# Gate and up projections of a second block's feed forwards as seven block products per pair of columns, with weights in pieces of 1024 columns

## The chip, the cores and the metric

The kernel runs on one core of a Trainium2 chip. The metric is device time in microseconds of one execution. PE is TensorE, DVE is VectorE, ACT is ScalarE, POOL is GpSimd, SP is SyncE, which issues the weight transfers here.

## The reference, cut to what matters

Two transformer blocks of two layers each run over 512 tokens of width 1024. Every layer ends in a feed forward of inner width 2816. The first block's has a causal convolution on the gate half, the second block's has none:

```python
def swiglu(h, w_gate_up, w_down):
    g, u = jnp.split(h @ w_gate_up, 2, axis=-1)
    return (jax.nn.silu(g) * u) @ w_down
...
        x = x + swiglu(rmsnorm_2(x, norm_ffn_g[layer]), ffn_w_gate_up[layer], ffn_w_down[layer])
```

Inputs, weights and output are float32.

## The kernel before

x lies transposed: 8 tiles of 128 features by 512 tokens. A float32 operand is split into a rounded half hi (ACT, L111 for weights) and a remainder lo (DVE, L112, which reads raw and hi from SBUF), and each product of tiles is three matmuls: hi by xh, hi by xl, lo by xh (`mm3`, L217 to L219). The norm's per-token factor Rb is multiplied in when a PSUM bank is read.

Weights come in chunks of 1024 rows by 256 columns (2048 columns in SBUF) in the order in which `make_plan` lists them. Three raw buffers and two hi/lo pairs rotate. `next` hands out a chunk; `pump`, called after every unit of 24 matmuls by `tick`, splits the chunk that follows in four pieces of 512 columns and loads ahead on SP's queue. `tick` then reads the finished bank (the `ev` functions) and lets each background generator (`bg`, `step`) do one step.

`ffn` goes over the 22 inner tiles of 128 in three parts (`FPARTS`, 8, 8 and 6 tiles). For each pair of tiles it takes a gate chunk `fa` and a value chunk `fv`, each as two units of 8 row tiles by 3 matmuls of 512 columns. `ev_a` multiplies by Rb (DVE, L870), applies silu (ACT, L880) and multiplies by Rb again (POOL, L881); `ev_v` multiplies by the value (DVE, L885) and splits the result (L229, L230). After a part the down chunks `fd` multiply its tiles and `x_add` adds to x (DVE, L536). The first pair of a feed forward straddles the norm (`first_pair`, `norm_gen`). The last layer's last part is `down_final`, in halves of 256 tokens, so with matmuls of 256 columns, and with the output behind it.

Every engine runs its instructions in the order of the program. The tile framework puts in the waits: an instruction waits for the tiles that it reads, and for the readers of a buffer that it overwrites. PSUM has eight banks, handed out in turn.

## Time and profile before

| | us |
|---|---|
| median of 3 runs | 2755.0 (2753.39 to 2757.13) |
| the profiled execution | 2753.09 |
| its span, first to last instruction | 2751.3 |
| PE busy in the span | 2719.3 |
| DVE, ACT, POOL busy | 1483.1, 1047.7, 335.6 |
| mean granted TensorE clock | 0.997 |

The span is what the trace shows; 1.8 us of the execution lie outside it. A matmul's own duration overlaps the next one's, so the price of a matmul is read from start to start. The feed forwards of the second block start at about 1650 and 2350 us of the span.

### The profile page before, as it was taken

Reading aid. Unit: us, or ns where it says so; the run is one execution under the profiler, and the core shown is the slowest. Engines: PE = TensorE matmul, PEld = TensorE weight load, DVE = VectorE, ACT = ScalarE, POOL = GpSimd, SP = SyncE. Lnnn points to the kernel's source line nnn. Section 1 sums busy time; section 2 is a strip of 40 time slices with the busy share of each in tenths; the row PEclk is TensorE's granted clock in tenths of the full one; section 3 lists DMA queues with packets and bytes.
Section 4 is the critical chain, followed back from the end, with each engine's and each line's share of the span. In section 5 each row is a group of like instructions: output and inputs, shape, how many; then the busy total and the mean of one; then the engine's idle time right before and its main releaser. Section 6 shows DMA issues by size and latency. Waiting matters only on the chain.

```text
span 2751.3 us, 33428 instructions
## 1 busy us (share of the span) xinstructions
PE 2719.3 (99%) x13358; PEld 2265.2 (82%) x13358; DVE 1483.1 (54%) x2533; ACT 1047.7 (38%) x1967; POOL 335.6 (12%) x394
## 2 busy tenths in 40 slices
PE   9999999999999999999999999999999999999998
PEld 7788888888878888888888887888888888788887
DVE  5644764545555375645466666434466656543444
ACT  5353343323445334423343354222243536432223
POOL 1110210101111011100021102000111001100002
PEclk9999999999999999999999999999999999999999
DMA  5131323232323133223233223332232112322321
GB/s 190 62 93 54 115 92 103 87 101 82 115 65 84 63 100 107 98 88 106 85 100 111 93 76 127 99 100 92 81 99 78 62 47 85 115 92 95 105 85 54
DMA packets 254269, 253.55 MB, mean 92 GB/s; under 512 B 16384, under 2 KB 252160, under 8 KB 253600
## 3 DMA queue, kind: packets, MB, share of 16 engines
q1 hardware_dynamic: 251808, 245.68, 27.6%
q0 software_dynamic: 1296, 4.92, 0.5%
q8 instruction: 105, 1.72, 0.3%
q10 hardware_dynamic: 1008, 0.80, 0.1%
q14 instruction: 52, 0.43, 0.0%
HBM read 247.15 MB, written 2.10 MB: 91 GB/s over the span
## 4 chain that ended last, share of the span: by engine, by line
PE 93%; DVE 4%; ACT 2%; issue 1%; POOL 0%; DMA 0%; POOLq 0%; ACTq 0%; DVEq 0%
PE ps L217 28%; PE ps L218 28%; PE ps L219 28%; DVE lo L112 1%; PE ps L828 1%; PE ps L730 1%; PE ps L1436 1%; PE ps L673 1%; DVE x L536 0%; PE ps L1160 0%; PE ps L843 0%; PE ps L451 0%; PE ps L754 0%; PE ps L460 0%; ACT xh L232 0%
## 5 line engine op out<-in xcount | busy, mean ns | idle before, releaser
L217 PE MATMUL ps<-xh,hi 128*128 128x512 f32 x2224 | 872.9, 392 | 5.1 <-ACT hi L111 5.1
L219 PE MATMUL ps<-xh,lo 128*128 128x512 f32 x2224 | 866.8, 390 | 1.6 <-DVE lo L112 1.5
L218 PE MATMUL ps<-xl,hi 128*128 128x512 f32 x2224 | 866.5, 390 | 0.0
L112 DVE TENSOR_TENSOR lo<-raw,hi 128x512 fp32r<-128x512 f32 (+2 forms) x922 | 635.8, 746 | 157.9 <-ACT hi L111 156.5
L111 ACT ACTIVATE hi<-raw 128x512 fp32r<-128x512 f32 (+2 forms) x922 | 506.6, 618 | 323.5 <-PE ps L218 254.2
L217 PEld LDWEIGHTS ps<-xh,hi 128*128 128x128 f32 x2224 | 418.0, 188 | 93.7 <-ACT hi L111 5.9
L219 PEld LDWEIGHTS ps<-xh,lo 128*128 128x128 f32 x2224 | 417.8, 188 | 90.7 <-DVE lo L112 3.4
L218 PEld LDWEIGHTS ps<-xl,hi 128*128 128x128 f32 x2224 | 418.0, 188 | 85.2 <-issue 0.2
L218 PE MATMUL ps<-actl,hi 128*128 128x512 f32 (+1 forms) x752 | 282.4, 376 | 0.3 <-DVE actl L230 0.3
L217 PE MATMUL ps<-acth,hi 128*128 128x512 f32 (+1 forms) x752 | 282.5, 376 | 0.0
L219 PE MATMUL ps<-acth,lo 128*128 128x512 f32 (+1 forms) x752 | 282.3, 375 | 0.0
L536 DVE TENSOR_TENSOR x<-ps,x 128x512 f32<-128x512 f32 x136 | 93.4, 688 | 266.5 <-PE ps L219 266.5
L218 PEld LDWEIGHTS ps<-actl,hi 128*128 128x128 f32 x752 | 141.5, 188 | 26.1 <-DVE actl L230 0.5
L217 PEld LDWEIGHTS ps<-acth,hi 128*128 128x128 f32 x752 | 141.5, 188 | 25.7
L219 PEld LDWEIGHTS ps<-acth,lo 128*128 128x128 f32 x752 | 141.5, 188 | 25.5
L870 DVE TENSOR_TENSOR a<-ps,Rb 128x512 f32<-128x512 f32 x88 | 60.6, 691 | 180.6 <-PE ps L219 173.1
L417 POOL TENSOR_TENSOR sq<-sq,sq 128x512 f32<-128x512 f32 (+1 forms) x73 | 94.7, 1302 | 436.4 <-ACT sq L411 435.9
L881 POOL TENSOR_TENSOR y<-y,Rb 128x512 f32<-128x512 f32 x44 | 57.0, 1297 | 588.2 <-ACT y L877 588.2
L881 POOL TENSOR_TENSOR a<-a,Rb 128x512 f32<-128x512 f32 x44 | 58.0, 1321 | 571.2 <-ACT a L880 571.2
L217 PE MATMUL ps<-hi,xh 128*128 128x256 f32 x384 | 113.4, 295 | 0.0
L218 PE MATMUL ps<-lo,xh 128*128 128x256 f32 x384 | 108.5, 283 | 0.0
L232 ACT ACTIVATE xh<-x,prm 128x512 fp32r<-128x512 f32 x72 | 52.0, 725 | 148.3 <-DVE x L536 145.8
(367 smaller groups left out, 3157.3 us busy)
## 6 DMA issues: line engine op xcount, KB each, us to landing
raw<-in_w_up SPq DMA_DIRECT2D x44, 1024.0 KB, 5.1
raw<-in_ffn_w_gate_up SPq DMA_DIRECT2D x44, 1024.0 KB, 5.1
raw<-in_w_in SPq DMA_DIRECT2D x39, 1024.0 KB, 5.1
raw<-in_w_down SPq DMA_DIRECT2D x16, 1024.0 KB, 5.1
raw<-in_ffn_w_down SPq DMA_DIRECT2D x16, 1024.0 KB, 5.1
raw<-in_od_w_in SPq DMA_DIRECT2D x10, 1024.0 KB, 5.2
raw<-in_w_o SPq DMA_DIRECT2D x8, 1024.0 KB, 5.1
raw<-in_xattn_wkv SPq DMA_DIRECT2D x8, 1024.0 KB, 5.1
```

Source lines behind the costliest of these rows:

```text
L111: nc.scalar.activation(g(hi, d), g(raw, s), AF.Copy)
L112: nc.vector.tensor_tensor(g(lo, d), g(raw, s), g(hi, d).bitcast(F32), op=SUB)
L217: mm(out, lhsT=wh, rhs=xh, start=first, stop=False)
L218: mm(out, lhsT=wh, rhs=xl, start=False, stop=False)
L219: mm(out, lhsT=wl, rhs=xh, start=False, stop=last)
L232: nc.scalar.activation(hv, src, AF.Copy, scale=scale)
L417: (nc.vector if dve else nc.gpsimd).tensor_tensor(acc[to], acc[to], q, op=ADD)
L536: self.nc.vector.tensor_tensor(self.x[j], ps, self.x[j], op=ADD)
L673: nc.tensor.matmul(z[b][:, o:o + n], lhsT=k[rs, kt * P:(kt + 1) * P], rhs=q[rs, kt * P:S], start=(kt != 3), stop=False, skip_group_check=True)
L730: nc.tensor.matmul(po[rs, kt * P:S], lhsT=vb[:, kt, h * 64:(h + 1) * 64], rhs=ag[kt], start=(kt == 0), stop=(kt == 3))
L870: nc.vector.tensor_tensor(t, ps, self.Rb, op=MUL)
L881: nc.gpsimd.tensor_tensor(t, t, self.Rb, op=MUL)
```

## The change

Only the second block's feed forwards compute differently. Their first two pairs of tiles stay as they were; for f from 4 on (`PLAIN`), the four blocks of a pair (gate and value columns by the upper and lower 512 rows) and the four blocks of the normalised x (upper and lower rows by the first and second 256 tokens) are combined by the scheme of Winograd's form of Strassen's product: seven products of blocks with sums before and after, in place of eight.

- The x side is formed once per feed forward by `factors`, a background generator: per j one scaling of two tiles by ACT, their multiplication by Rb and four sums of 256 columns on POOL, then splits on ACT and DVE. It is stepped in the ticks of the pairs 0 and 2, and yields `ready` after six steps.
- The weight side is formed for every pair by `schunks`: POOL sums in place on the raw tiles (`pre` two, `post1` one, `post5` one, 1024 columns each), and seven splits of 1024 columns, one for each product.
- `product` runs 24 matmuls of 256 columns on a bank. `spair` reads the banks: copies by ACT, sums by DVE, silu by ACT, and half of the multiplication by the value on POOL. The seventh product of a pair runs behind the first of the next, or behind the first down unit of a part.
- All weights of the kernel, in every stage, come in units of 1024 columns: six raw buffers and four hi/lo pairs of that size, one ACT and one DVE instruction per unit, `pump` by units.
- All down-projections but the last come as pieces of 2 row tiles by 512 columns, with four banks open at a time. There are four parts instead of three, of 6, 6, 4 and 6 tiles, in the last feed forward 6, 6, 6 and 4.
- Pools are opened and closed by stage, and the bias table of the first block is loaded twice.

```diff
+    RAW, HL = 6, 4
...
+    def may_emit(self):
+        i = self.emitted
+        if i >= len(self.units) or i >= self.limit:
+            return False
+        held = sum(1 for k in range(self.base, i) if not self.units[k]["own"])
+        return self.units[i]["own"] or held < self.HL
+    def pump(self, n=None):
+        n = self.pace if n is None else n
+        while n > 0 and self.may_emit():
+            self._emit()
+            n -= 1
+        while self.loaded < min(len(self.raws), self.freed + self.RAW):
+            self._load()
+    pace = 2
...
+def schunks(name, w, c1, c2):
+    b = [block(w, r, 4, c, 256) for r, c in ((0, c1), (0, c2), (512, c2), (512, c1))]
+    b11, b12, b22, b21 = b
+    box = {}
+    def add(c, to, x, y):
+        c.nc.gpsimd.tensor_tensor(to, x, y, op=ADD)
+    def pre(c, r):
+        box["t"] = c.pf.tile([P, 1024], F32, tag="t0", bufs=1, name=c.nm("t0")).rearrange("p (k c) -> p k c", k=4)
+        add(c, box["t"], r[0], r[1])
+        add(c, r[1], r[1], r[2])
+    def post1(c, r):
+        add(c, r[0], r[0], r[1])
+    def post5(c, r):
+        add(c, r[0], r[0], r[1])
+    def temp(c, hi, lo, raws):
+        c.put(hi, lo, box.pop("t"))
+    u = [dict(unit(4, 256, whole, (b11,), 0), pre=pre, praws=(b11, b12, b22), post=post1),
+         unit(4, 256, temp, (b11,), 0),
+         unit(4, 256, whole, (b11,), 0),
+         unit(4, 256, whole, (b22,), 1),
+         dict(unit(4, 256, whole, (b21, b11), 1, 1), post=post5, praws=(b21, b11)),
+         unit(4, 256, whole, (b12,), 1),
+         unit(4, 256, whole, (b21,), 1)]
+    out = [chunk(name, [], [x]) for x in u]
+    out[0]["raws"] = b
...
-FPARTS = ((0, 8), (8, 16), (16, 22))
-def ffn_plan(wu, wd):
-    pl = []
-    for f0, f1 in FPARTS:
+FPARTS = ((0, 6), (6, 12), (12, 16), (16, 22))
+FPARTS_END = ((0, 6), (6, 12), (12, 18), (18, 22))
+PLAIN = (22, 4)
...
+    pairs = {f: schunks("fs", wu, 2816 + 128 * f, 128 * f) for f in range(PLAIN[b], 22, 2)}
+    parts = FPARTS_END if end else FPARTS
+    for f0, f1 in parts:
         for f in range(f0, f1, 2):
-            pl.append(wchunk("fa", wu, 0, 8, 128 * f))
-            pl.append(wchunk("fv", wu, 0, 8, 2816 + 128 * f))
-        for i in range(4):
-            pl.append(wchunk("fd", wd, 128 * f0, f1 - f0, 256 * i))
+            if f < PLAIN[b]:
+                pl.append(wchunk("fa", wu, 0, 8, 128 * f))
+                pl.append(wchunk("fv", wu, 0, 8, 2816 + 128 * f))
+                continue
+            c = pairs[f]
+            if not first:
+                pl += c[:1] + late
+            pl += c[1:6]
+            late, first = c[6:], []
+        if end and f1 == 22:
+            pl += late
+            for i in range(4):
+                pl.append(wchunk("fd", wd, 128 * f0, f1 - f0, 256 * i))
+            continue
+        for i in range(2):
+            for f in range(f0, f1, 2):
+                pl.append(chunk("fd", [block(wd, 128 * f, 2, 512 * i, 512)], [unit(2, 512)]))
+                if i == 0 and f == f0:
+                    pl += late
+                    late = []
+                    if f1 - f0 == 4 and f1 >= PLAIN[b]:
+                        first = pairs[f1][:1]
+                        pl += first
...
+    def factors(self):
...
+        two, last, rest = None, None, []
+        self.ready = False
+        for j in range(5):
+            cur = None
+            if j < 4:
+                xa, xb = self.t("xa"), self.t("xb")
+                for t, k in ((xa, j), (xb, j + 4)):
+                    nc.scalar.activation(t, self.x[k], AF.Copy, scale=self.ngain(k))
+                    tt(t, t, self.Rb, op=MUL)
+                a11, a21, a12, a22 = xa[:, H[0]], xa[:, H[1]], xb[:, H[0]], xb[:, H[1]]
+                s14, s23 = self.t("s14"), self.t("s23")
+                tt(s14[:, H[0]], a22, a21, op=SUB)
+                tt(s23[:, H[0]], a11, s14[:, H[0]], op=ADD)
+                tt(s23[:, H[1]], a21, a11, op=SUB)
+                tt(s14[:, H[1]], s23[:, H[0]], a12, op=SUB)
+                cur = a11, xb, s14, s23
+            if last:
+                a11, xb, s14, s23 = last
+                if j % 2:
+                    two = self.ft("Ah"), self.ft("Al")
+                put(a11, ("11",), tiles=two, at=256 * ((j - 1) % 2))
+                put(s14, ("1", "4"))
+                put(s23, ("2", "3"), scale=-1.0)
+                rest.append(xb)
+            last = cur
+            yield
+        self.ready = True
+        for xb in rest:
+            yield
+            put(xb, ("12", "22"))
...
+    def product(self, ps, key, first):
+        hi, lo = self.next("fs")
+        mm = self.nc.tensor.matmul
+        A = self.A[key]
+        for nt in range(2):
+            o = ps[:, 256 * nt:256 * nt + 256]
+            for j in range(4):
+                wh, wl = (w[:, j, nt * P:nt * P + P] for w in (hi, lo))
+                xh, xl = A[j]
+                for i, (w, x) in enumerate(((wh, xh), (wh, xl), (wl, xh))):
+                    mm(o, lhsT=w, rhs=x, start=(first and nt == 0 and j == 0 and i == 0), stop=(j == 3 and i == 2), skip_group_check=True)
+        self.pump(1)
+        self.step()
...
+        def spair(f, ah, al):
+            A, D, B = (self.ps() for _ in range(3))
+            half = lambda t, nt: t[:, H[nt]]
+            self.product(A, "11", True)
+            yield
+            s1 = self.t("s1")
+            nc.scalar.copy(s1, A)
+            self.product(D, "1", True)
+            self.settle()
+            p5 = self.t("p5")
+            nc.scalar.copy(p5, D)
+            self.product(A, "2", False)
+            a = [self.t("a") for _ in range(2)]
+            self.product(D, "4", False)
+            d = self.t("d")
+            nc.scalar.copy(d, D)
+            for nt in range(2):
+                nc.vector.scalar_tensor_tensor(a[nt][:, H[0]], half(A, nt), -1.0, half(d, nt), op0=MUL, op1=SUB)
+            self.finish(gf)
+            self.product(B, "12", True)
+            nc.vector.tensor_tensor(s1, B, s1, op=ADD)
+            self.product(A, "3", False)
+            for nt in range(2):
+                nc.vector.scalar_tensor_tensor(a[nt][:, H[1]], half(A, nt), -1.0, half(p5, nt), op0=MUL, op1=SUB)
+            g = [act_a(a[nt], f + nt, False) for nt in range(2)]
+            for nt in range(2):
+                nc.gpsimd.tensor_tensor(g[nt][:, H[0]], g[nt][:, H[0]], half(s1, nt), op=MUL)
+            yield
+            self.product(A, "22", False)
+            def out():
+                for nt in range(2):
+                    nc.vector.tensor_tensor(g[nt][:, H[1]], half(A, nt), g[nt][:, H[1]], op=MUL)
+                for nt in range(2):
                     h, lo = self.split(g[nt], "act")
                     ah.append(h)
                     al.append(lo)
-                if first:
-                    self.first_pair(self.next("fa"), ev_a, self.norm_gen())
-                    first = False
-                else:
-                    self.pair("fa", ev_a)
-                self.pair("fv", ev_v)
-            if end:
-                after[0]()
-            ks = range(f1 - f0)
+            self.later.append(out)
...
+                        if plain < 22:
+                            gf = self.bg(self.factors())
+                    else:
+                        self.pair("fa", ev_a)
+                    self.pair("fv", ev_v)
+                    if f + 2 == plain < 22:
+                        while not self.ready:
+                            self.step()
+                        self.xh = self.xl = None
+                    continue
+                g = started
+                if g is None:
+                    g = spair(f, ah, al)
+                    next(g)
+                    if last is not None:
+                        end_of(last)
+                next(g)
+                last, started = g, None
...
+                ps = [self.ps() for _ in range(4)]
+                if end and c:
+                    hls = [self.next("fd", hold=u > 0) for u in range(0, n, 2)]
+                    for nt in range(4):
+                        for u in range(0, n, 2):
+                            hi, lo = hls[u // 2]
+                            for k in range(2):
+                                w = (slice(None), k, slice(nt * P, nt * P + P))
+                                self.mm3(ps[nt], hi[w], lo[w], ah[u + k], al[u + k], u + k == 0, u + k == n - 1)
+                            if nt == 3:
+                                self.base += 1
+                                self.pump(1)
+                        self.x_add(4 * c + nt, ps[nt])
+                        self.step()
+                    break
+                for u in range(0, n, 2):
+                    hi, lo = self.next("fd")
+                    for nt in range(4):
+                        for k in range(2):
+                            w = (slice(None), k, slice(nt * P, nt * P + P))
+                            self.mm3(ps[nt], hi[w], lo[w], ah[u + k], al[u + k], u + k == 0, u + k == n - 1)
+                        if nt == 1:
+                            self.pump(1)
+                        if u + 2 == n:
+                            self.x_add(4 * c + nt, ps[nt], norm=end)
+                            self.step()
+                    self.pump(1)
                     self.step()
-                    continue
-                for nt in range(2):
-                    p = self.ps()
-                    self.unit(p, hl, nt, ks, xs=(ah, al))
-                    self.pump()
-                    add(2 * i + nt, p)
-                    self.step()
+                    if u == 0 and c == 0:
+                        if last is not None:
+                            end_of(last)
+                            last = None
+                        if end:
+                            after[0]()
+                            self.A = None
+                        if n == 4 and f1 >= plain:
+                            started = spair(f1, *lists[i + 1])
+                            next(started)
+                        self.settle()
```

## Rows read from the trace of the kernel before

**Rows 1.** Busy table: busy us (share of span) x instructions.

```profile
PE 2719.3 (99%) x13358; PEld 2265.2 (82%) x13358; DVE 1483.1 (54%) x2533; ACT 1047.7 (38%) x1967; POOL 335.6 (12%) x394
```

**Rows 2.** PE's waits, whole span: waiting line, releaser: us, times, longest.

```profile
PE ps L217 <- ACT hi L111: 5.1, 1, 5.1
PE ps L451 <- DVE sq L417: 4.7, 1, 4.7
PE ps L219 <- DVE lo L112: 3.6, 5, 0.7
...
PE ps L218 <- DVE actl L230: 0.3, 1, 0.3
```

**Rows 3.** Windows: length, busy (count) of PE, PEld, DVE, ACT, POOL, clock, DMA.

```profile
1690.00:1720.00 30.00, 30.00 (x134) 24.83 (x133) 17.21 (x27) 9.80 (x18) 3.19 (x4) 1.00 0.33 105
1433.00:1436.00 3.00, 3.00 (x15) 3.00 (x16) 2.62 (x6) 0.67 (x2) 0.00 (x0) 0.50 0.01 3
1436.00:1441.00 5.00, 5.00 (x24) 5.00 (x25) 4.07 (x25) 0.00 (x0) 0.00 (x0) 0.50 0.66 210
1443.00:1446.00 3.00, 3.00 (x28) 3.00 (x27) 1.96 (x4) 2.56 (x5) 0.00 (x0) 1.00 0.00 0
```

**Rows 4.** Timeline of PE, last feed forward: start, duration, instruction; two runs' ends.

```profile
2659.93 0.39 PE L219 MATMUL ps<-xh,lo 128*128 128x512 f32 x1
...
2700.72 0.39 PE L219 MATMUL ps<-xh,lo 128*128 128x512 f32 x1
...
2729.78 0.28 PE L217 MATMUL ps<-acth,hi 128*128 128x256 f32 x1
...
2738.30 0.28 PE L219 MATMUL ps<-acth,lo 128*128 128x256 f32 x1
```

**Rows 5.** Groups by line and shape: busy us, mean ns of one, idle before.

```profile
L411 ACT ACTIVATE sq<-x 128x512 f32<-128x512 f32 x80 | 48.7, 616 | 0.0
L1657 ACT ACTIVATE sq<-x 128x256 f32<-128x256 f32 x16 | 6.6, 416 | 17.4 <-DVE x L1655 17.3
L232 ACT ACTIVATE xh<-x,prm 128x512 fp32r<-128x512 f32 x72 | 52.0, 725 | 148.3 <-DVE x L536 145.8 <-DMA x<-in_xT 1.3 <-DMA prm<-in_prm 1.1
L1655 DVE TENSOR_TENSOR x<-ps,x 128x256 f32<-128x256 f32 x16 | 6.7, 422 | 14.1 <-PE ps L219 14.0
L1661 POOL TENSOR_TENSOR sq<-sq,sq 128x256 f32<-128x256 f32 x12 | 8.9, 742 | 34.4 <-ACT sq L1657 34.2
```

**Rows 6.** Timeline, feed forward: four weight splits and a POOL multiply, each undisturbed.

```profile
1698.10 2.49 DVE L112 TENSOR_TENSOR lo<-raw,hi 128x512 fp32r<-128x512 f32 x4
1702.31 1.30 POOL L881 TENSOR_TENSOR a<-a,Rb 128x512 f32<-128x512 f32 x1 [12.18 <-ACT a L880]
```

**Rows 7.** Timeline of DVE and POOL where both have work.

```profile
1103.81 1.22 DVE L112 TENSOR_TENSOR lo<-raw,hi 128x512 fp32r<-128x512 f32 x1
1104.95 1.23 DVE L112 TENSOR_TENSOR lo<-raw,hi 128x512 fp32r<-128x512 f32 x1
...
1103.42 1.07 POOL L417 TENSOR_TENSOR sq<-sq,sq 128x256 f32<-128x256 f32 x1
1104.56 1.07 POOL L417 TENSOR_TENSOR sq<-sq,sq 128x256 f32<-128x256 f32 x1
...
1675.44 0.68 DVE L536 TENSOR_TENSOR x<-ps,x 128x512 f32<-128x512 f32 x1
...
1675.41 1.29 POOL L417 TENSOR_TENSOR sq<-sq,sq 128x512 f32<-128x512 f32 x1 [4.44 <-ACT sq L411]
```

**Rows 8.** Timeline of DVE: readers that waited for two value units' ends.

```profile
1695.50 0.69 DVE L885 TENSOR_TENSOR a<-ps,a 128x512 f32<-128x512 f32 x1 [0.83 <-PE ps L219]
...
1717.26 0.69 DVE L885 TENSOR_TENSOR a<-ps,a 128x512 f32<-128x512 f32 x1 [3.02 <-PE ps L219]
```

**Rows 9.** Timeline of PE: a norm's sums, with the wait before them.

```profile
1432.59 3.58 PE L451 MATMUL ps<-ones,sq 128*128 128x1 f32 x16 [4.75 <-DVE sq L417]
```

More of the change, by code (lines that the diff above doesn't have):

```diff
@@ new lines, in _emit @@
+        u["split"](self, hi, lo, [self.raw[r] for r in u["raws"]])
+        self.hl[i] = (hi, lo)
+        self.emitted += 1
+        if "post" in u:
+            u["post"](self, [self.raw[r] for r in u["praws"]])
+        for r in u["raws"][u["keep"]:u["keep"] + u["frees"]]:
+            self.raw.pop(r, None)
+            self.freed += 1
+        if self.emitted < len(self.units) and "pre" in self.units[i + 1]:
+            n = self.units[i + 1]
+            while self.loaded <= max(n["praws"]):
+                self._load()
+            n["pre"](self, [self.raw[r] for r in n["praws"]])
@@ new lines, with next @@
+    pace = 2
+    def next(self, name, ticks=2, hold=False):
+        i = self.cur
+        c = self.chunks[i]
+        assert c["name"] == name, (c["name"], name)
+        first, n = c["first"], len(c["units"])
+        if not hold:
+            self.base = first
+        while self.emitted < first + n:
+            self._emit()
+        self.cur = i + 1
+        self.pace = 1 if ticks > 2 else 2
+        self.limit = len(self.units)
+        got = [self.hl.pop(first + k) for k in range(n)]
+        if n == 1:
+            return got[0]
+        per = c["units"][0]["kc"]
+        return Tall([g[0] for g in got], per), Tall([g[1] for g in got], per)
@@ L251, in slice_k, with whole @@
     return (slice(None), slice(a, b), slice(None))
-def chunk(name, dma, kc, rc, oc=None, split=None, zero=None):
-    return dict(name=name, dma=dma, kc=kc, rc=rc, oc=oc or rc, split=split, zero=zero, own=False)
-def wchunk(name, w, r0, kc, c0, nc_=256):
-    src = w[r0:r0 + kc * P, c0:c0 + nc_].rearrange("(k p) c -> p k c", p=P)
-    return chunk(name, [(slice_k(0, kc), src)], kc, nc_)
+def whole(c, hi, lo, raws):
+    if isinstance(hi, Parts):
+        for i in range(len(hi.tiles)):
+            c.put(hi.tiles[i], lo.tiles[i], raws[0][:, 2 * i:2 * i + 2])
+    else:
+        c.put(hi, lo, raws[0])
@@ new lines, in in_parts, with f, raw, unit @@
+def in_parts(parts, zero=None):
+    g = lambda t, v: v(t) if callable(v) else t[v]
+    def f(c, hi, lo, raws):
+        if zero:
+            c.nc.gpsimd.memset(hi[zero].bitcast(F32), 0.0)
+            c.nc.gpsimd.memset(lo[zero].bitcast(F32), 0.0)
+        for d, s in parts:
+            c.put(g(hi, d), g(lo, d), g(raws[0], s))
+    return f
+def raw(dma, kc, rc):
+    return dict(dma=dma, kc=kc, rc=rc)
+def unit(kc, oc, split=whole, raws=(0,), frees=1, keep=0):
+    return dict(kc=kc, oc=oc, split=split, raws=raws, frees=frees, keep=keep)
@@ new lines, in chunk, with block, wchunk @@
+def chunk(name, raws, units):
+    return dict(name=name, raws=raws, units=units, own=False)
+def block(w, r0, kc, c0, nc_):
+    src = w[r0:r0 + kc * P, c0:c0 + nc_].rearrange("(k p) c -> p k c", p=P)
+    return raw([(slice_k(0, kc), src)], kc, nc_)
+def wchunk(name, w, r0, kc, c0, nc_=256, split=whole):
+    per = 1024 // nc_
+    raws = [block(w, r0 + k * P, min(per, kc - k), c0, nc_) for k in range(0, kc, per)]
+    return chunk(name, raws, [unit(r["kc"], nc_, split, (i,)) for i, r in enumerate(raws)])
```

362 lines of the change are left out of this document (185 added, 177 removed).

## The prediction

> **What bounds the kernel now.** I read the busy table first: TensorE (PE) is busy 99% of the span, VectorE (DVE) 54%, GpSimd (POOL) 12% [rows 1]. Busy PE is not PE at its peak, so I looked next at what PE waits for. The list of PE's waits is short, its longest entries are single events at the start and at norms, and no weight transfer delays PE after the start; the wait of 0.3 us for the last activation split before the final down-projection is the only one in a feed forward tail that matters here [rows 2]. The windows view of the second block's first feed forward has PE busy for all 30 us at a granted clock of 1.00 while DVE is busy for 17.2 and POOL for 3.2 [rows 3]. So PE's own matmul stream sets the time and everything else hides under it. A change that takes matmuls away gains their time, as long as the engines that feed PE keep up. That second half is the question here: the change gives DVE and POOL far more to do, and POOL's share rises most.
>
> **What a matmul costs.** Start to start in the timeline is the price. 180 intervals of 128x512 matmuls run from 2659.93 to 2700.72, 0.2266 us each; 71 intervals of 128x256 ones, each with a weight load of its own, from 2729.78 to 2738.30, 0.1200 us each [rows 4]. Halving the columns costs 0.120 rather than 0.113.
>
> **Part 1, seven products for eight (removes PE time).** A pair of gate and value columns was 2 x 2 x 8 x 3 = 96 matmuls of 512 columns: 21.75 us. A product is 2 x 4 x 3 = 24 matmuls of 256 columns, 2.88 us; seven are 168, 20.16 us. Per pair 1.59 us go; f = 4 to 20 in both layers is 18 pairs: -28.7 us. The last layer's final part has 4 row tiles in place of 6, so its 256-column matmuls fall from 288 to 192 and 48 of 512 columns come elsewhere: 34.56 against 23.04 + 10.88, -0.6. Together **-29.3 us**. The Trainium skill, page "TensorE: Matmul & The Clock Gate", section "Back-to-back issue gap", gives an isolated gap of columns/2.4 ns plus 2.5, which is 215.8 and 109.2 ns and would make the pairs save an estimated 43 us. The rows are slower by 11 ns at either size, and the measurement decides.
>
> **Part 2, what the feeding engines now do.** Durations at 1024 columns stand in no row; I extend the step from 256 to 512 columns. ACT 0.416 and 0.616 give 1.02; DVE 0.42 and 0.68 give 1.20; POOL 0.74 [rows 5] and 1.30 [rows 6] give 2.42. Per pair the splits go from 8 x 512 columns to 7 x 1024, on ACT and on DVE, and POOL gets four sums of 1024 (9.7 us) and two products of 256 (1.5) for its old two multiplies by Rb (2.6).
>
> DVE and POOL don't run side by side. Where POOL adds 256 columns while DVE splits 512, a split that takes 2.49/4 = 0.62 us alone [rows 6] takes 1.22, ending 0.54 after POOL's end; and POOL's add takes 1.07 for 0.74, ending 0.60 after DVE's end [rows 7]. They take turns, one instruction each. An add of DVE that reads PSUM is not held: 0.68 us right through a POOL add [rows 7]. So held time is 0.60 for POOL at 256 columns, 1.16 at 512 and 2.28 at 1024; for DVE 0.28, 0.55 and 1.08. Per pair: POOL 4 x 2.28 + 2 x 0.60 = 10.3, DVE 7 x 1.08 + 2 x 0.55 = 8.7, together 19.0 of 20.16 us, and DVE has 3.2 us of PSUM reads more in the same queue. The Trainium skill, page "SBUF — State Buffer", section "Who interferes with whom", says that a DVE instruction with two SBUF inputs and a GpSimd instruction that reads SBUF exclude each other for the whole instruction. That speaks against this change, whose POOL sums are the longest of the kernel; the trace agrees at 256 and 512 columns, and no row has 1024.
>
> **Part 3, the factor stage (adds a stall).** factors() runs in the ticks of three plain units groups (fv 0, fa 2, fv 2) and must be through before the first product. Let 0 be the end of the first fv unit, 1695.50 - 5.44; the last fv unit ends at 27.2 [rows 8], and the product needs its fourth factor 9 matmuls later, 28.3. POOL's queue from 4.1 on (ACT's scaling, 0.72 each [rows 5], stands behind the first unit's own split): one factor step is 2 x 1.30 + 4 x 0.74 = 5.6. In program order: steps 1 and 2, the two sums of the first pair's `pre` (4.84), Rb 1.30, step 3, Rb 1.30, step 4. Alone it has the first piece of step 4 at 4.1 + 5.6 + 5.6 + 4.8 + 1.3 + 5.6 + 1.3 + 1.3 = 29.6 and ends at 33.8: with two splits behind each, waits of 2.4 us in the first product and 1.8 in the second. That is the lower bound, **4 us**. With turns, DVE's SBUF work in that time goes between: two fv splits of 1024 (+1.9), three sets of factor splits (+3.5), the first two product weights (+1.9), activations (+0.8). ACT's queue is chained in, since the weight splits stand behind factor splits that wait for POOL. The last factor is then split at about 42.3, 14 us after PE wants it. PE then idles long enough to lose its clock: after the 4.75 us wait at a norm [rows 9] the granted clock is 0.50, the 1.2 GHz level, through the windows to 1441, and 1.00 again from 1443 [rows 3]: some 8 us at half speed, 4 us. I take 14 + 4 per layer, the walk by the measured turns, **+36 us** for two; bounds 8 and 48 (a further turn behind a 2.3 us sum, and its matmuls at half clock, for each).
>
> **Part 4, the steady pairs (a wait that takes the place of none).** PE's order in a pair is the products 11, the former pair's 22, then 1, 2, 4, 12, 3, one every 2.88 us from 0. Bank A holds 11 and 2; DVE must read it, with d from product 4, before product 3 writes it. Product 4 ends at 14.4, ACT's copy of d takes 0.62 (as any ACT pass over 512 columns [rows 5]), so the reader can start at 15.2; product 3 is due at 17.28. In front of the reader DVE has, from 8.1 (the fifth weight's buffer comes free at 5.76, then ACT 1.02 and DVE 1.20): two activation splits, the splits of the sixth own weight and of the next pair's first. POOL has, from 8.1: the sum after the fifth weight, and the two sums of the next pair. Taking turns: POOL to 10.5, DVE 11.05, POOL 13.35, DVE 13.9, POOL 16.2, DVE 17.3 and 18.5, then the two reads of A to 19.4. PE waits 2.1 us. A pair whose successor's sums don't fall into it (the last of each part) has no such wait, so it is 5 pairs of 9 in each layer: 10 x 2.1 = **+21 us**; bounds 0 (cover holds) and 33 (half as much again, since the next pair starts DVE 1.4 late).
>
> **Part 5, the rest.** In the last layer the last pair's product 22 follows its product 3 on the same bank with nothing between (two reads of A, 0.84 and their hand-over), and the final down-projection starts with 6 matmuls, 0.72 us, of cover for the last pair's multiply, split and split (0.42 + 0.42 + 0.62 + 0.68) where 12 and an earlier half covered it before [rows 2, 5]: **+3**, bounds 0 and 5. Costed at nothing: eight more x additions per feed forward (0.68 each, hidden by 5.44 us down units); the bias table loaded a second time, by POOL's queue at the start of the second mixer, whose first reader comes tens of microseconds later (uncovered it would be a few us); twice as many loads of half the size on SP (it waits for DVE to free buffers, PE for no load); splits of 1024 in all other stages (first half 0.4 us later, fixed parts saved), bounds -4 and +5, norm ends included.
>
> **Sum.** -29.3 + 36 + 21 + 3 = +30.7. The profiled execution has 2751.3 in its span and 1.8 outside, 2753.1; with the change 2783.8. The median of the runs is 1.9 above that execution, so **2786 us**.
>
> **Rivals.** First, faster: POOL's long sums do not hold DVE as the short ones do (it gets in early, or the sums come while DVE has nothing ready). Then only POOL's own length counts: -29.3 + 8 + 3 = -18, 2737 us; with every stall hidden, 2726. For it: DVE and POOL together still fit, 19.0 of 20.16. Against it: the turns in rows 7. It decides as soon as DVE reaches bank A before 16.4. Chance 0.28. Second, one walk holds and the other doesn't: the steady waits of 21 with 8 in the factor stage, +3, 2758 us (0.12); or 36 in the factor stage with steady waits hidden, +10, 2765 us (0.10). Third, it doesn't do what it says, because the weight load bounds a 256-column matmul: a load is busy for 2265.2/13358 = 0.17 us [rows 1], which one after the other is 168 x 0.17 = 28.5 a pair, 6.7 more than before, +121 and 2876 us without any stall; against it, 71 matmuls with a load each kept 0.120 [rows 4]. Chance 0.01.
>
> **How the numbers follow.** The forecast has 0.49, with its own range 2768 to 2806 (the bounds of parts 3 to 5, not all at once). A measurement of this kernel tells 0.2%, 5.5 us, from no change. Faster 0.28; within 0.12; slower 0.49 + 0.10 + 0.01 = 0.60. The range that leaves 2 in 10 out runs from 2730, most of the first rival, to 2806.
>
> **What would show it.** Right: PE idle for over 10 us before the first product of each layer, waiting for a factor split, with a granted clock of 0.50 after it; DVE's 1024-column splits at over 2 us beside POOL sums; PE waits of about 2 us at product 3 for DVE's read of A, in pairs that have a successor. Product matmuls 0.120 apart confirm part 1. Wrong: splits at 1.2 us throughout, PE busy 99% in the product stages, or a factor stage whose wait is below 5 us: then the time falls under 2750.

## The result, and the profile after

The changed kernel takes 2786.1 us in the median (2784.8 to 2788.0), the one before 2756.0 in the runs beside it (2753.4 to 2757.1): 1.0111 of before, 95% interval 1.0094 to 1.0129. The profiled execution's span grew by 32.9 us, from 2751.3 to 2784.2. The forecast was 2786.

The head of the page and one of its costliest groups (line, engine, operation, count | busy us, mean ns | idle time before them):

```profile
span 2784.2 us, 36548 instructions
PE 2706.2 (97%) x14606; PEld 2312.0 (83%) x14606; DVE 1636.6 (59%) x2266; ACT 1116.8 (40%) x1684; POOL 571.9 (21%) x517
...
L133 DVE TENSOR_TENSOR lo<-raw,hi 128x1024 fp32r<-128x1024 f32 (+3 forms) x519 | 662.8, 1304 | 279.9 <-ACT hi L132 277.3
```

Against [rows 1], PE is busy for 13 us less and idle for 46 us more (78.0 against 32.0). What it waits for now (line of the waiter, whom it waited for: us in total, times, longest), the first seven entries:

```profile
PE ps L1049 <- ACT hi L132: 13.5, 2, 7.7
PE ps L1049 <- DVE a L1094: 9.9, 5, 2.0
PE ps L225 <- ACT hi L132: 9.4, 2, 7.5
PE ps L1049 <- DVE Al L993: 7.7, 4, 3.1
PE ps L1049 <- DVE lo L133: 5.5, 2, 2.7
PE ps L580 <- DVE ry L560: 3.9, 2, 2.4
PE ps L1049 <- ACT Ah L992: 3.3, 2, 2.0
```

L1049 is the matmul of a product, so its entries have nothing to answer to in [rows 2]. Four of them (ACT hi, DVE Al, DVE lo, ACT Ah) are the factor stages, 13.5 + 7.7 + 5.5 + 3.3 = 30.0 us in two layers; another, 9.9, is the read of bank A in steady pairs. L225 is the ordinary hi matmul; 7.5 of its 9.4 are the start of the kernel, 5.1 in [rows 2].

**The factor stage of the first layer.** PE's waits in time (start, duration, instruction, [idle before, released by]), then the clock there (stretch, its length, then busy us and number of PE, PEld, DVE, ACT, POOL; then the granted clock):

```profile
1729.99 0.58 PE L1049 MATMUL ps<-Ah,hi 128*128 128x256 f32 x1 [7.70 <-ACT hi L132]
1733.53 0.58 PE L1049 MATMUL ps<-Ah,lo 128*128 128x256 f32 x1 [2.75 <-DVE lo L133]
1737.34 0.58 PE L1049 MATMUL ps<-Ah,hi 128*128 128x256 f32 x1 [1.96 <-ACT Ah L992]
1740.97 0.58 PE L1049 MATMUL ps<-Al,hi 128*128 128x256 f32 x1 [3.05 <-DVE Al L993]
1755.80 0.39 PE L1049 MATMUL ps<-Al,hi 128*128 128x256 f32 x1 [1.33 <-DVE Al L993]
```

```profile
1722.00:1730.00 8.00, 0.30 (x3) 0.01 (x1) 3.42 (x5) 4.33 (x8) 7.84 (x8) 0.65 0.00 0
1730.00:1742.00 12.00, 4.24 (x15) 3.37 (x16) 11.24 (x9) 3.38 (x6) 10.15 (x8) 0.50 0.00 0
1742.00:1746.00 4.00, 4.00 (x24) 4.00 (x24) 1.56 (x4) 3.12 (x5) 0.00 (x0) 0.63 0.00 0
1746.00:1750.00 4.00, 4.00 (x36) 4.00 (x35) 3.94 (x6) 4.00 (x7) 0.00 (x0) 1.00 0.00 0
```

PE idles for 16.8 us here, in the five waits shown, and for 13.2 in the second layer. POOL is busy for 18 of the first 20 us. The granted clock falls to 0.50, the 1.2 GHz level, and is back by 1746. PE's busy time at the low clock, taken times what the clock lacks of 1, is what the half speed cost: 4.24 x 0.50 + 4.00 x 0.37 = 3.6 us, and 3.4 in the second layer.

The first entry is worth following. PE waits there for ACT's half of the first product's weight. ACT's queue, and POOL's, just ahead of it:

```profile
1727.08 0.72 POOL L1013 TENSOR_TENSOR s<-s,xb 128x256 f32<-128x256 f32 x1
...
1727.84 0.63 ACT L992 ACTIVATE Ah<-s 128x512 fp32r<-128x512 f32 x1 [3.23 <-POOL s L1013]
1728.37 0.61 ACT L995 ACTIVATE Ah<-s 128x512 fp32r<-128x512 f32 x1
1728.89 1.04 ACT L132 ACTIVATE hi<-raw 128x1024 fp32r<-128x1024 f32 x1
```

That weight needs no sum; it stands behind a factor split which waits for POOL's third factor step. So the name in the list of waits is a weight's, and the cause is POOL's queue, two steps back.

**A steady pair.** DVE, POOL and ACT around the wait at 1832.98 (1.98 us, product 3 for DVE's read of A at L1094):

```profile
1822.87 4.82 DVE L238 TENSOR_TENSOR actl<-a,acth 128x512 fp32r<-128x512 f32 x2 [0.43 <-ACT acth L237]
1827.61 4.56 DVE L133 TENSOR_TENSOR lo<-raw,hi 128x1024 fp32r<-128x1024 f32 x2
1832.09 0.74 DVE L1094 SCALAR_TENSOR_TENSOR a<-ps,d 128x256 f32<-128x256 f32 x2
...
1821.90 2.42 POOL L327 TENSOR_TENSOR raw<-raw,raw 128x1024 f32<-128x1024 f32 x1 [3.82 <-issue]
1824.26 2.88 POOL L327 TENSOR_TENSOR t<-raw,raw 128x1024 f32<-128x1024 f32 x1
1827.21 2.74 POOL L327 TENSOR_TENSOR raw<-raw,raw 128x1024 f32<-128x1024 f32 x1
1832.31 2.37 POOL L327 TENSOR_TENSOR raw<-raw,raw 128x1024 f32<-128x1024 f32 x1 [2.36 <-DVE lo L133]
...
1828.16 0.59 ACT L1092 COPY d<-ps 128x512 f32<-128x512 f32 x1 [1.89 <-PE ps L1049]
```

d is there at 1828.8. DVE reads A at 1832.1, since two activation splits and two weight splits before it take 9.2 us beside three sums of POOL. The two reads themselves take 0.74 us, from PSUM, although the next sum starts beside them.

### The profile page after: what moved, and what is told of

It reads as the page before. It is cut to its first block, busy times and chain, and to the rows that moved or that the text cites. A ratio compares the mean times of both kernels' runs of the same rounds, so it can differ in the third digit from the quotient of the medians.

```text
span 2784.2 us, 36548 instructions
## 1 busy us (share of the span) xinstructions
PE 2706.2 (97%) x14606; PEld 2312.0 (83%) x14606; DVE 1636.6 (59%) x2266; ACT 1116.8 (40%) x1684; POOL 571.9 (21%) x517
## 4 chain that ended last, share of the span: by engine, by line
PE 85%; DVE 5%; issue 3%; ACT 3%; POOL 2%; DMA 0%; POOLq 0%; ACTq 0%; SPq 0%; DVEq 0%
PE ps L225 22%; PE ps L227 22%; PE ps L226 22%; PE ps L1049 11%; DVE lo L133 2%; PE ps L948 1%; ACT hi L132 1%; PE ps L850 1%; PE ps L1722 1%; PE ps L793 1%; PE ps L874 1%; DVE x L656 0%; PE ps L1448 0%; PE ps L963 0%; DVE xl L241 0%
## 5 line engine op out<-in xcount | busy, mean ns | idle before, releaser
L133 DVE TENSOR_TENSOR lo<-raw,hi 128x1024 fp32r<-128x1024 f32 (+3 forms) x519 | 662.8, 1304 | 279.9 <-ACT hi L132 277.3
L225 PE MATMUL ps<-xh,hi 128*128 128x512 f32 x1648 | 649.4, 394 | 7.5 <-ACT hi L132 7.5
L227 PE MATMUL ps<-xh,lo 128*128 128x512 f32 x1648 | 643.6, 391 | 0.9 <-DVE lo L133 0.8
L226 PE MATMUL ps<-xl,hi 128*128 128x512 f32 x1648 | 643.0, 390 | 0.0
L132 ACT ACTIVATE hi<-raw 128x1024 fp32r<-128x1024 f32 (+3 forms) x519 | 510.6, 1012 | 302.4 <-PE ps L226 223.5
L225 PEld LDWEIGHTS ps<-xh,hi 128*128 128x128 f32 x1648 | 310.3, 188 | 73.1 <-ACT hi L132 7.5
L1049 PE MATMUL ps<-Ah,hi 128*128 128x256 f32 x1008 | 290.5, 288 | 27.8 <-ACT hi L132 13.5
L1049 PE MATMUL ps<-Al,hi 128*128 128x256 f32 x1008 | 289.5, 287 | 7.7 <-DVE Al L993 7.7
L1049 PE MATMUL ps<-Ah,lo 128*128 128x256 f32 x1008 | 289.2, 287 | 5.5 <-DVE lo L133 5.5
L225 PE MATMUL ps<-acth,hi 128*128 128x512 f32 (+1 forms) x736 | 280.1, 381 | 1.0 <-ACT acth L237 1.0
L1049 PEld LDWEIGHTS ps<-Ah,hi 128*128 128x128 f32 x1008 | 197.3, 196 | 31.7 <-ACT hi L132 25.1
L1049 PEld LDWEIGHTS ps<-Al,hi 128*128 128x128 f32 x1008 | 197.3, 196 | 9.2 <-DVE Al L993 8.7
L1049 PEld LDWEIGHTS ps<-Ah,lo 128*128 128x128 f32 x1008 | 197.2, 196 | 6.1 <-DVE lo L133 6.1
L225 PEld LDWEIGHTS ps<-acth,hi 128*128 128x128 f32 x736 | 138.5, 188 | 27.3 <-ACT acth L237 1.4
```

What stands on the lines that cost most here:

```text
L132: self.nc.scalar.activation(hi, raw, AF.Copy)
L133: self.nc.vector.tensor_tensor(lo, raw, hi.bitcast(F32), op=SUB)
L225: mm(out, lhsT=wh, rhs=xh, start=first, stop=False)
L226: mm(out, lhsT=wh, rhs=xl, start=False, stop=False)
L227: mm(out, lhsT=wl, rhs=xh, start=False, stop=last)
L1049: mm(o, lhsT=w, rhs=x, start=(first and nt == 0 and j == 0 and i == 0), stop=(j == 3 and i == 2), skip_group_check=True)
```

## Experiments

Each run changes the kernel after the change, and its ratio is to the kernel before, from executions on the same chip. Medians of before in these groups were 2754.6 to 2755.8 us.

### The rewrite with plain pairs only (e1_all_plain)

```diff
-PLAIN = (22, 4)
+PLAIN = (22, 22)
...
-                end_of(last)
+                if last is not None:
+                    end_of(last)
                 return self.down_final(ah, al)
```

> All pairs of the second block go the plain way (eight block products): no factors, no sums of weights; the other edits (weights of 1024 columns, down-projections by 2 rows x 512, the new parts of the feed forward) stay. Theory (what the changed kernel loses, it loses in the factor stage and the steady pairs): the rest of the rewrite costs little, as the stages ahead of the second block's feed forward come out 5 to 7 us later in the changed kernel; 2755 to 2765 us, 1.000 to 1.003 of before, TensorE idle some 35 to 45 us in all. Rival (the 1024-column weights and the new down-projections cost the time themselves, and the products only show it): 2780 us or more, with no wait at a product.

Measured: 2759.0 us, 1.0012 (1.0003 to 1.0021). Weights of 1024 columns, the new parts and the new down-projections cost 3 to 4 us together; the products and what feeds them cost the other 27, net of what they save.

### Products one pair later (e2_factors_later)

```diff
-PLAIN = (22, 4)
+PLAIN = (22, 6)
```

> One more plain pair stands ahead of the first product (products from f = 6 on rather than 4), so that GpSimd and VectorE get 21.75 us more for the factors; 2 of 18 pairs lose their saving of 1.59 us. Theory: the 30 us of waits in the two factor stages go, and with them the 7 us that the matmuls at half clock cost there; the five waits of 2.0 us in the steady pairs stay: 2786 - 30 - 7 + 3 = 2752 us, 0.997 to 1.001 of before. Rival (the queues of VectorE and GpSimd are full anyway, so the wait is only put off to the first pairs): 2775 us or more, waits of over 10 us a layer left at the products.

Measured: 2764.9 us, 1.0037 (1.0026 to 1.0049), between the two. The 30 us at the products are gone, but the plain pair that stands ahead of them now waits, in both layers; in the first:

```profile
1725.10 0.50 PE L225 MATMUL ps<-xh,hi 128*128 128x512 f32 x1 [2.68 <-ACT hi L132]
1728.83 0.79 PE L227 MATMUL ps<-xh,lo 128*128 128x512 f32 x1 [2.84 <-DVE lo L133]
```

With 1.54 and 3.03 in the second layer that is 10.1 us, and some 4 us of half clock behind them: 2786 - 30 - 7 + 3 + 10 + 4 = 2766. That is neither the theory's time nor the rival's: time for the factors was given, but they were still issued in a heap, in front of the plain weights in the queues of ACT and DVE.

### GpSimd as long busy, but reading nothing (e3_fill_same_length)

```diff
     def add(c, to, x, y):
-        c.nc.gpsimd.tensor_tensor(to, x, y, op=ADD)
+        for part in (slice(0, 4), slice(0, 4), slice(0, 2)):
+            c.nc.gpsimd.memset(to[:, part], 0.5)
```

> GpSimd's four sums of weights for each pair become fills of the same tiles with a constant, 2.5 fills of 1024 columns for a sum, so that GpSimd is as long busy (0.957 us a fill in the trace of before, 2.4 us a sum) but reads nothing; the weights of five products are then not the right ones. Theory (a sum that reads two operands and a VectorE instruction with SBUF inputs take turns): VectorE's 1024-column splits fall from 1.30 us in the mean to under 1.15, the five waits of 2.0 us for the read of bank A go, the factor stages wait for 8 to 20 us in all rather than 30: 2750 to 2772 us. Rival (GpSimd's length alone sets it): splits in the mean unchanged, the five waits and the factor waits stay, 2782 to 2790 us.

Measured: 2763.5 us, 1.0030 (1.0018 to 1.0041). The five waits of 2.0 us for the read of A are gone (one of 0.9 us at the end, for another read, is left), although POOL's fills take 175 us in all, as much as 72 sums of 2.42. DVE beside fills, in the factor stage:

```profile
1715.98 0.43 DVE L994 TENSOR_TENSOR Al<-xa,Ah 128x256 fp32r<-128x256 f32 x1 [1.63 <-ACT Ah L993]
1716.50 0.69 DVE L994 TENSOR_TENSOR Al<-s,Ah 128x512 fp32r<-128x512 f32 x1
...
1714.89 2.54 POOL L328 MEMSET t<- 128x1024 f32 x3
1717.37 2.55 POOL L328 MEMSET raw<- 128x1024 f32 x3
```

In the changed kernel the same two splits stand beside the sums:

```profile
1715.69 1.61 DVE L993 TENSOR_TENSOR Al<-xa,Ah 128x256 fp32r<-128x256 f32 x1 [1.64 <-ACT Ah L992]
1717.23 2.88 DVE L993 TENSOR_TENSOR Al<-s,Ah 128x512 fp32r<-128x512 f32 x1
...
1714.61 2.41 POOL L327 TENSOR_TENSOR t<-raw,raw 128x1024 f32<-128x1024 f32 x1
1717.10 2.45 POOL L327 TENSOR_TENSOR raw<-raw,raw 128x1024 f32<-128x1024 f32 x1
```

So what holds DVE's splits is a sum that reads, not POOL being busy. The Trainium skill, page "SBUF — State Buffer", section "Who interferes with whom", states this: a VectorE instruction with two SBUF inputs contends with a GpSimd instruction that reads SBUF, and not with one that only writes it. The trace agrees on both halves.

Two of my numbers were off: the splits' mean fell only to 1.27 us, since an undisturbed one takes 1.23 and not the 1.15 that I allowed; and the factor stages still wait for 21.5 us. Most of their wait is therefore not the weight sums' hold but the factor steps themselves, on POOL and in the queues behind it.

### Reads of A ahead of the next split (e4_read_a_first)

```diff
-            self.product(D, "4", False)
+            self.product(D, "4", False, pump=False)
...
                 nc.vector.scalar_tensor_tensor(a[nt][:, H[0]], half(A, nt), -1.0, half(d, nt), op0=MUL, op1=SUB)
+            self.pump(1)
```

(with `pump=False`, `product` leaves out its own `self.pump(1)`)

> In each pair VectorE's two reads of bank A (after product 4) are issued ahead of the split of the next pair's first weight, in place of behind it. Nothing else changes. Theory: the reads no longer queue behind a split that GpSimd's sums hold, and the five waits of 2.0 us at product 3 go, with the 4 us of half clock after two of them: 2786 - 14 = 2772 us (2768 to 2778). Rival (VectorE is short of time in the pair, so another step comes late instead, such as the next pair's first weight): 2783 us or more, with waits at another product.

Measured: 2779.7 us, 1.0089 (1.0074 to 1.0104): about half of the 14 us that I gave, between theory and rival. Four waits of 0.8 us are left at product 3, and at product 22, whose read is L1102 here, there are ten of 0.3 to 0.9 where one was (they add to 3.3 and 3.7 us). What stands ahead of the read now is one split:

```profile
1828.50 3.42 DVE L133 TENSOR_TENSOR lo<-raw,hi 128x1024 fp32r<-128x1024 f32 x1
1831.85 0.74 DVE L1095 SCALAR_TENSOR_TENSOR a<-ps,d 128x256 f32<-128x256 f32 x2
```

### Gain and Rb on VectorE (e5_rb_on_vector)

```diff
-                    nc.scalar.activation(t, self.x[k], AF.Copy, scale=self.ngain(k))
-                    tt(t, t, self.Rb, op=MUL)
+                    nc.vector.scalar_tensor_tensor(t, self.x[k], self.ngain(k), self.Rb, op0=MUL, op1=MUL)
```

> In the factor steps one VectorE instruction takes gain and Rb together (one of 0.68 us for each of 8 tiles a layer) in place of a ScalarE scaling and a GpSimd multiply of 1.30 us; the sums of the factors stay on GpSimd. Theory (GpSimd's queue sets when the factors are there): a factor step on GpSimd shrinks from 5.6 to 3.0 us, so the last factor comes some 10 us sooner in each layer; the 30 us of waits in the factor stages fall to 5 to 15, the five waits of 2.0 us stay: 2763 us (2756 to 2775). Rival (the held time of VectorE sets it, and that grows by 4 x 1.4 us a layer): 2780 us or more.

Measured: 2775.1 us, 1.0071 (1.0057 to 1.0085), at the slow end of what I gave; the factor stages wait for 19.0 us instead of 30.0, more than the 5 to 15 that I gave. POOL's queue is part of the cause. The five waits stay at 9.9.

### First sums issued later (e8_sums_and_reads)

```diff
+        if "pre" in u:
+            while self.loaded <= max(u["praws"]):
+                self._load()
+            u["pre"](self, [self.raw[r] for r in u["praws"]])
         n = u["kc"] * u["oc"]
...
-        if self.emitted < len(self.units) and "pre" in self.units[i + 1]:
...
```

(with the edit of e4_read_a_first)

> As the run that issues the reads of bank A first, and besides GpSimd's two first sums of a pair's weights are issued right ahead of that pair's own first split, no longer behind the split of the weight before it: in a steady pair they then come behind the reads of A, and before the first pair behind the next factor step. Theory: the reads no longer stand behind a split held by those sums, so the 7 us of short waits at products 3 and 22 that were left fall to 0 to 2; and the factors come up to 4.8 us sooner in each layer: 2763 us (2757 to 2772). Rival (the pair has no time left on VectorE and GpSimd, so another weight comes late instead; or the sums come late for product 1): 2777 us or more.

Measured: 2780.3 us, 1.0090 (1.0076 to 1.0104). My theory fell in both places. In steady pairs the four waits of 0.8 us stayed, and so did the sums: at f = 8 they start at 1821.50, 1823.86 and 1826.80, and in e4_read_a_first, where the pair stands 1.31 us later, at 1822.81, 1825.18 and 1828.11. POOL had been idle for 3.8 us before them in both. On an empty queue it made no difference where the program puts a sum among the work of other engines. In the factor stage the sums did come later and made the wait that the rival named. PE's longest wait is 8.86 us, for a factor split of ACT. It stands behind ACT's split of the summed weight t, and behind an activation split that waits for DVE, whose own split of t comes first:

```profile
1731.79 2.34 POOL L326 TENSOR_TENSOR t<-raw,raw 128x1024 f32<-128x1024 f32 x1
...
1734.16 1.06 ACT L131 ACTIVATE hi<-t 128x1024 fp32r<-128x1024 f32 x1 [8.80 <-POOL t L326]
```

### These edits together (e9_all_three, e10_three_and_later)

> The two edits together: VectorE takes gain and Rb in the factor steps; the reads of A and GpSimd's first sums are reordered. Theory: both groups of waits go and the saving of the products is left: 2786 - 30 (factor waits) - 7 (half clock there) - 14 (short waits and half clock behind them) = 2735 us, 0.993 of before (2733 to 2748). Rival (what is taken from one queue comes back in another): over 2755 us.

Measured: 2770.4 us, 1.0054 (1.0040 to 1.0067). The rival came: the wait for t, as above, keeps 21.5 us in the factor stages.

> As the run with the two edits together, and the products begin one pair later (from f = 6). Theory: the plain pair more costs 1.59 us a layer and hides what is left of the factor wait: 2738 us (2735 to 2745), faster than the run with the two edits only if that one still waits over 3 us for factors. Rival (ScalarE's queue, where the weights of the plain pair stand behind factor splits, holds that pair as it did when only the start of the products was moved, 10 us): 2750 us or more.

Measured: 2754.9 us, 0.9999 (0.9990 to 1.0008), no different from before; the rival came here too. The plain pair still waits for 3.7 and 1.9 us, and in the steady pairs the many short waits of e4_read_a_first are left.

### ScalarE frees bank A (e11_scalar_frees_a, e12_spread_and_copy)

```diff
-            self.product(A, "2", False)
+            a2, a3 = self.t("a2"), self.t("a3")
+            self.product(A, "2", False, a2)
...
-                nc.vector.scalar_tensor_tensor(a[nt][:, H[0]], half(A, nt), -1.0, half(d, nt), op0=MUL, op1=SUB)
+                nc.vector.scalar_tensor_tensor(a[nt][:, H[0]], half(a2, nt), -1.0, half(d, nt), op0=MUL, op1=SUB)
```

(the same for product 3 and a3; `product` copies the bank to its last argument by ACT ahead of `pump`)

> Only the steady pairs are changed: right after products 2 and 3 ScalarE copies bank A to SBUF (0.57 us each), and VectorE forms its two differences from the copies, so that bank A no longer waits for VectorE's queue. Theory (the waits at products 3 and 22 come from where VectorE's reads of A stand in its queue, behind splits that GpSimd's sums hold): no wait at a product for VectorE's differences, 9.9 us of idle and some 4 us of half clock gone: 2772 us (2768 to 2777); the factor stages wait for their 30 us as before. Rival (VectorE and GpSimd have no time left in the pair, so that the differences, now held by GpSimd too, make another step late): 2781 us or more.

Measured: 2799.2 us, 1.0162 (1.0147 to 1.0178), 13 us worse than the change. The wait for DVE's read is gone, and others stand in its place. The factor stages wait for 34.6 us, 4.6 more, and in the steady pairs and at the ends of parts there are now:

```profile
PE ps L1049 <- DVE lo L133: 9.3, 6, 2.7
PE ps L225 <- ACT acth L237: 7.8, 2, 4.7
PE ps L1049 <- ACT p L1089: 3.9, 9, 0.9
```

(4 of the 6 waits of the first entry, 3.8 us, belong to steady pairs.) One reason shows in one instruction. Here the two differences read SBUF, beside a sum of POOL, and further on (last line) with none beside them:

```profile
1838.15 2.96 DVE L1097 SCALAR_TENSOR_TENSOR a<-a,d 128x256 f32<-128x256 f32 x2
...
1838.37 2.45 POOL L327 TENSOR_TENSOR raw<-raw,raw 128x1024 f32<-128x1024 f32 x1 [2.36 <-DVE lo L133]
...
1933.84 0.75 DVE L1097 SCALAR_TENSOR_TENSOR a<-a,d 128x256 f32<-128x256 f32 x2
```

In the steady pair above they read A from PSUM and take 0.74 us beside the start of a sum. So a copy that frees a bank turned 0.7 us of DVE, which the sum did not hold, into 3.0. How much of the 13 us this makes is not measured. In the wait of 4.7 us PE wants an activation split that stands in ACT's queue behind the split of a down weight, and that one waits 4.15 us for its load; why the load comes late I did not settle.

> Four edits: ScalarE copies bank A as in the run that does that alone; the products begin at f = 6; VectorE takes gain and Rb in the factor steps; and the first three factor steps are issued at every other tick, so that they spread over the plain pairs of f = 0 to 4 and no plain weight stands behind a row of factor splits. Theory: the factor stages wait for under 4 us in all and the pairs for none, so the plain-pairs kernel less its savings is left: 2759 - 16 x 1.59 - 0.6 = 2733, plus some 3 at the end: 2736 us, 0.993 of before (2731 to 2744). Rival (the short waits come back elsewhere in VectorE's queue, about 6 us a layer, as in the run with three edits): 2748 us or more.

Measured: 2756.8 us, 1.0007 (0.9999 to 1.0016): the rival. No wait is left in either factor stage; the short waits of e11_scalar_frees_a are left in the steady pairs and at the ends of parts.

### The factors spread out (e14_factors_spread)

```diff
             last = cur
             yield
+            if j < 3:
+                yield
```

(with the edit of e5_rb_on_vector, and products from f = 6)

> The factor stage alone is changed, in three ways: products from f = 6 on, VectorE takes gain and Rb in the factor steps, and the first three factor steps are issued at every other tick. The steady pairs stay as in the changed kernel. Theory (the factor stage's loss is a crowd on GpSimd, VectorE and ScalarE's queue, and a crowd that is spread out costs nothing): no wait over 0.5 us at a plain pair or a first product; the five waits of 2.0 us stay, with some half clock behind them: 2765 (products from f = 6 alone) - 10 (its waits) - 4 (half clock there) = 2751 us (2746 to 2756). Rival (the crowd takes the same time wherever it stands, so a wait comes up at a plain pair): 2759 us or more.

Measured: 2751.8 us, 0.9986 (0.9977 to 0.9996), as the theory had it. The first entry of PE's waits is the read of A; no wait at a plain pair or first product is left:

```profile
PE ps L1050 <- DVE a L1095: 9.9, 5, 2.0
```

### Activation splits later (e15_splits_late)

```diff
-                for nt in range(2):
-                    h, lo = self.split(g[nt], "act")
...
+                splits.append(sp)
...
                 nc.vector.scalar_tensor_tensor(a[nt][:, H[1]], half(A, nt), -1.0, half(p5, nt), op0=MUL, op1=SUB)
+            late()
```

(with the edits of e14_factors_spread and e4_read_a_first; `late` runs the splits kept back)

> As the run that spreads the factors, and in the steady pairs VectorE's reads of A go ahead of the next pair's first split, while the two activation splits of the pair before go behind the reads that follow product 3 (in a part of 4 row tiles behind the reads that follow product 4). Theory: VectorE has some 2 us without work there in each pair, so what is left of the short waits goes down to 0 to 2 us a layer: the plain-pairs kernel less its savings, 2759 - 16 x 1.59 - 0.6, plus some 4: 2737 us, 0.993 of before (2733 to 2747). Rival (the short waits come up at another step, as they did when ScalarE copied bank A): 2752 us or more.

Measured: 2743.0 us, 0.9956 (0.9943 to 0.9968). It beats both kernels, the one before by 0.4%. Its span is 2740.9 us, and the wait for the reads of A is now:

```profile
PE ps L1050 <- DVE a L1106: 3.5, 6, 2.0
PE ps L227 <- DVE lo L133: 2.9, 5, 1.1
...
PE ps L225 <- ACT acth L237: 2.2, 2, 1.7
```

Against the plain-pairs kernel it saves 16 of the 25 us that 16 pairs could (16 x 1.59). The 0.6 us of the shorter last part, which my expectation took off as well, that kernel has saved already: its parts are those of the changed kernel.

## Why the prediction was right, and where it was not

The table sets each term beside the trace. Of a stretch in a feed forward the loss is the sum over its matmuls of the time to the next start beyond 0.2266 or 0.1200 us, waits and half clock included; before lost 0.6 us in all this way.

| term | foretold us | measured us |
|---|---|---|
| 1, matmuls | -29.3 | the pace held, so -29.3 by count |
| 3, factor stages | +36 | +38.5 (21.1 and 17.4) |
| 4, steady pairs | +21 | +17.2 (10.4 and 6.8) |
| 5, end of the feed forwards | +3 | +3.5, by difference |
| 5, the rest | 0 | +3.0 (+4.7 ahead of the second block's first feed forward, -1.7 between its two) |
| sum | +30.7 | +32.9 |

The plain-pairs run checks the two large terms from outside: the products cost 27 us net of the 28.7 that they save by count, which makes 55.7, and parts 3 and 4 lose 38.5 + 17.2 = 55.7. That the sum came out within 2.2 us is in part luck, since +2.5, -3.8, +0.5 and +3.0 nearly cancel. The 1.9 us that I put on for the median then covered those 2.2: the changed kernel's median lies only 0.1 above its profiled execution of 2785.95.

**Part 1** held: from 1846 to 1912, 277 intervals of 256 columns add to 33.23 us, 0.1200 each; the rival of the weight load is out.

**Part 2** held. The lengths extended to 1024 columns were right: undisturbed rows are 1.23 for DVE's split, 1.04 to 1.06 for ACT's and 2.37 to 2.42 for POOL's sum, against 1.20, 1.02 and 2.42. An undisturbed split, in the first pair of a part:

```profile
1800.67 1.23 DVE L133 TENSOR_TENSOR lo<-raw,hi 128x1024 fp32r<-128x1024 f32 x1 [2.36 <-ACT hi L132]
```

That DVE and POOL take turns at this length too, and that it is the reading which holds, is shown by fills that do not hold the splits, and by a subtraction that is held only when it reads SBUF beside a sum. The first rival, long sums that don't hold, is out.

**Part 3** was right in size, 30.0 us of idle time and 7.0 of half clock against 28 and 8, and right in its chain, POOL to ACT's queue to the weights. In form it differed: no wait of over 10 us ahead of the first product, but four within that product, the longest 7.7, and that one for a weight; the fifth, of 1.33 us, stands in the fifth product. How much of it is turns I put too boldly: 10 of the 14 us of a layer. With fills for the weight sums, which takes away their turns and leaves those of the factor steps, 10.8 of 15.0 us a layer stay; the rest of that split is not measured, so a total that came out says little for the walk's two shares. One turn shows by itself: the wait of 3.05 us at 1740.97 is for a factor split that stands behind an instruction of DVE held for 3.03 us, shown in the last section, and with fills it is 0.72. The stage can be had without a wait: one pair more leaves 10 us (e2_factors_later), one pair more with the steps spread and Rb on DVE leaves none (e14_factors_spread). That the heap is the cause, and not the work that Rb puts on POOL, fits these runs but is not shown apart, since no run spreads the steps with Rb left on POOL. Spreading without the extra pair was not tried either.

**Part 4** had the right mechanism and length, 1.98 against 2.1 us, at product 3, for that read. The count was wrong, five and not ten. The walk put the former pair's two activation splits into every pair's queue. The first pair of a part has none of them there, as they went with the part's end. Only pairs with both a pair before them in the part and a successor wait: f = 8, 14 and 18 in the first layer, 8 and 14 in the second. In the first layer f = 14 ends a part, and I had counted it out; but in a part of four tiles the next pair's first product is started early, so its sums fall into f = 14. That is 10.7 us with the matmul's restart; half clock after two of them added 3.3, which I had costed at nothing, and waits under 0.7 us the rest. Two errors of opposite sign, half the count and no half clock, came out 4 us low.

**Part 5** was costed at 3 and measured 3.5, inside its bounds; the rest came out at +3.0, also inside. The plain-pairs run shows some 3 to 4 us without any product. The start makes part of it: PE's first wait is 7.5 us in the changed kernel (7.0 with plain pairs), 5.1 before, so 2.4 of the 4.7 are there from the start. What adds the others is not traced.

**The other way out.** The runs show that the sign was not the idea's but the schedule's: with the same seven products, in 16 pairs in place of 18, and the factors, reads and splits placed otherwise, the time falls 12 us under before. What my expectations of the repairs missed, in seven runs, is that a repair in one queue brings up the next wait (e2, e4, e8, e9, e10, e11, e12).

## What to carry to other kernels

Before moving sums to an engine that seems idle, ask what it reads and beside whom: the turns of two engines can be walked with durations from shorter rows, and here the walk gave the sign and length of the steady pairs' wait, though not how many pairs have it. Follow a wait back through the in-order queues; the instruction that is named may be late only because of what stands ahead of it, and a background job that fits in total can still stop the work that stands behind it in a queue. Moving an instruction in the program did nothing on an engine whose queue is empty there.

## What the runs showed of the hardware

- A DVE instruction with one SBUF input was held too. In the factor stage of the changed kernel one on 512 columns took 3.03 us beside a sum. In the kernel before, with POOL idle, the same instruction takes 0.42 (at 1713.82). In the run with fills (last line) it took 0.70 beside a fill, so this one is slower beside a fill too, which the splits are not:

```profile
1737.56 3.03 DVE L1511 TENSOR_SCALAR r<-r 128x512 f32<-128x512 f32 x1
...
1737.05 2.80 POOL L327 TENSOR_TENSOR raw<-raw,raw 128x1024 f32<-128x1024 f32 x1
...
1736.43 0.70 DVE L1512 TENSOR_SCALAR r<-r 128x512 f32<-128x512 f32 x1
```

- The clock can fall after a wait of 2 us: of the five equal waits of 1.98 us, two were followed by a granted clock of 0.50 for some 3 us (1834.00 to 1836.00 is all at 0.50), and three were not. Ahead of each, PE's matmuls had kept their pace for 15 us but for at most one gap of 0.2. The same five waits of 1.98 us stand in three of the experiments: the clock fell after one of them in e2_factors_later, after none in e5_rb_on_vector, after two in e14_factors_spread. Every time it was the wait at f = 8 of a layer. What tells these from the others is open.

```profile
1834.00:1836.00 2.00, 2.00 (x12) 2.00 (x11) 2.00 (x2) 0.00 (x0) 0.68 (x1) 0.50 0.07 25
```
